# VectorE in GpSimd's place for the elementwise work of a hybrid mixer and mixture-of-experts block

## Chip and metric

One core of one Trainium2 chip. The metric is the device time of one execution in microseconds, the median of several runs. TensorE (PE) multiplies matrices out of SBUF into PSUM; VectorE (DVE) and ScalarE (ACT) read and write both; GpSimd (POOL) works on SBUF only and also issues the indirect DMAs; SyncE (SP) issues most other DMAs.

## What is computed

One layer of a hybrid block on 1024 tokens of width 1024, with 16 learnt tokens in front, all in float32:

```
h   = layer_norm([meta; x])
q,f,i,g,... = split(h @ w_in)                     # 9224 columns
y_a = head_norm(hgrn2(q, 1-f, i, log f)) * silu(g_a)          # 8 heads of 128
y_b = head_norm(mlstm(conv q, conv k, v)) * sigmoid(o_b)      # 4 heads
h   = layer_norm(alpha*h + (sigmoid(gate_a)*(y_a @ w_a) + sigmoid(gate_b)*(y_b @ w_b)) @ w_out)
out = layer_norm(alpha*h + routed_experts(h, top 8 of 64) + shared_expert(h))
```

HGRN2 is a gated linear recurrence: scores between a query at t and a key at s carry, for each of 128 channels, the product of the forget gates between s and t.

## The kernel before

**Precision and weights.** A float32 product is made of three matmuls of a faster format: each operand is a high part plus a low part, and high x high, high x low and low x high are added up in PSUM (`mm3`, L134 to L136). A weight piece of 128x1024 comes by DMA into a `wraw` tile, ScalarE copies it into the high part `wh` (L195), and the low part is raw minus high, `wl` (L196). `split_weights` does this for a list of pieces; `on_pool` names those whose low part GpSimd makes. `load_slab` splits four pieces, a slab of 512 columns, with high priority, so ahead of their use, and gives GpSimd pieces 1 and 3 (`SLAB_POOL`). The six pieces of the shared expert are split in the same way, 1, 3 and 5 of them on GpSimd (`SHARED_POOL`). The experts of the routed part never use GpSimd for this (`POOL_SPLITS` is empty, L1505).

**Stages.** The embedding makes the first norm and transposes it (L282 to L348); its own low parts and bias sums on GpSimd (L283, L325) are outside the change. Then for two halves of the HGRN part: a slab IA, a slab GA, a slab of f, one of q, and four heads. A slab goes through TensorE tile by tile into one of three PSUM banks `mm`, and from there through a staging tile to DRAM; heads load their parts from there. Then come VB and OB, the convolution, four mLSTM heads with the branch gates, the branch and output products by halves of the tokens with the second norm (`Tokens.norm`, L160 to L162), routing and the shared expert, the loop over 95 blocks of expert tokens, and the last norm.

**Gates.** `gate_out` (L413 to L425) turns a tile of GA into silu times a row of norm weights, a tile of OB into sigmoid times such a row. ScalarE writes the sigmoid to a staging tile (L419); for silu it also copies the PSUM tile to a second one (L422), and GpSimd multiplies twice (L423, L424) before SP's DMA to DRAM.

**A head.** `hgrn_head` builds the scores by doubling: at level lv blocks of B = 2^lv steps pair up. With `pre` the running product of gates within a block and `suf` that to a block's end, a level makes `qp` = query x pre of the odd blocks (L725), `ks` = key x suf of the even blocks (L727), 8 small matmuls (L739), a masked write of the scores (L742, or two ScalarE copies from level 5 on), the new suffix (L756) and the new prefix (L757). Level 0 is short (L719 to L721), level 6 ends the suffixes (L753, L754). Of levels 1 to 6 GpSimd makes the keys except at level 6 (`KS_DVE`), and of levels 1 to 5 the suffixes except at level 5 (`SUF_DVE`). Before the levels the diagonal is taken (L700 to L707); after them transposes, the chunk states (L779, L782), the output matmuls (L791, L792) into a PSUM tile `po` of which there is one, and the head norm (L794 to L799).

**Order.** The framework plans the order of instructions on each engine at build time, by priority in program order and by its own estimates of durations, and each engine then runs its list in that order, waiting on semaphores. A few parts are excepted, where the order is that of the program: PE and DVE in the embedding, PE in the branch and output stage and the first half of the token stage, PE, POOL and SP in the expert loop. In the heads all engines are planned, so a projection's matmuls fill the places between those of a head as the plan has them.

Of the kernel before, what the change touches and what calls it, by code (L numbers as in the profile page):

```python
# [14 lines left out]
AF = mybir.ActivationFunctionType  # L15
# [4 lines left out]
P = 128  # L20
D = 1024
KT = 8
# [22 lines left out]
KS_DVE = (6,)  # L45
SUF_DVE = (5,)
# [2 lines left out]
TAIL = (('A',1),('A',3),('S',0),('S',2),(('C0','C1'),()),('A',5),(('C2','C3','S4'),(0,1,2,3)),('F',0),('F',1),('A',7),('F',2),('F',3),('S',6),(('C4','C5','C6','C7'),(4,5,6,7)),('F',5),('F',4),('F',7),('F',6))  # L49
ADD_DVE = (3,5,7)  # L50
MUL_POOL = ()
ADD_POOL = (5,6,7)
SHARED_POOL = (1, 3, 5)
LATER = 300
RATE = 4.6
RATE_S = 3.0
# [9 lines left out]
SLAB_POOL = (1, 3)  # L66
# [4 lines left out]
def block_kernel(tc, A, out):  # L71
    nc = tc.nc
# [85 lines left out]
    def layer_norm(o, x, g, b, n, mul, add):  # L158
        sc = layer_norm_stats(x, n)
        nc.scalar.activation(o, x, AF.Identity, bias=sc[:n, 1:2], scale=sc[:n, 0:1])  # L160
        mul.tensor_mul(o, o, g[:n])
        add.tensor_add(o, o, b[:n])  # L162
# [22 lines left out]
    def split_weights(src, ahead, take=None, on_pool=()):  # L185

        res = []
        take = take or (lambda j: [wpool.tile([P, 1024], F32R, name="w" + q, tag="w" + q, bufs=6) for q in "hl"])
        with tc.high_priority(ahead) if ahead else ExitStack():
            for j, v in enumerate(src):  # L190
                raw = take_raw()
                dst = raw if len(v.shape) == 2 else raw.rearrange("p (k n) -> p k n", k=2)
                last.append(nc.sync.dma_start(dst, v))
                h, l = take(j)
                nc.scalar.activation(h, raw, AF.Copy)  # L195
                (nc.gpsimd if j in on_pool else nc.vector).tensor_sub(l, raw, h.bitcast(F32))  # L196
                res.append((h, l))
        return res
# [3 lines left out]
    def load_slab(src, c0):  # L202

        pairs = split_weights([src[k * 256:(k + 1) * 256, c0:c0 + 512].rearrange("(k p) n -> p k n", p=P)
                               for k in range(KT // 2)], 3000, on_pool=SLAB_POOL)
        hs = [t[:, c:c + 512] for t, _ in pairs for c in (0, 512)]
        ls = [t[:, c:c + 512] for _, t in pairs for c in (0, 512)]
        return hs, ls
# [40 lines left out]
    def stage_tile():  # L249
        return stage.tile([P, 512], F32, name="st", tag="st", bufs=6)  # L250
# [155 lines left out]
    def natural_slab(c0, emit, meta, slab=None):  # L406
        slab = slab or load_slab(w_in, c0)
        for i in range(NT):
            emit(proj_n(slab, NM + i * P, P), NM + i * P, P)
        if meta:  # L410
            emit(proj_n(slab, 0, NM), 0, NM)

    def gate_out(dst, c0, src, silu):  # L413
        row = stage.tile([P, 512], F32, name="nrow", tag="nrow", bufs=1)
        nc.sync.dma_start(row, bass.AP(tensor=src.tensor, offset=src.offset + c0, ap=[[0, P], [1, 512]]))

        def emit(pm, t0, n):
            s = stage_tile()
            nc.scalar.activation(s, pm, AF.Sigmoid)  # L419
            if silu:  # L420
                x = stage_tile()
                nc.scalar.activation(x, pm, AF.Copy)  # L422
                nc.gpsimd.tensor_mul(s, s, x)  # L423
            nc.gpsimd.tensor_mul(s, s, row)  # L424
            nc.sync.dma_start(dst[t0 - NM:t0 - NM + n, c0:c0 + 512], s)  # L425
        return emit

# [13 lines left out]
    def f_slab(s):  # L441
        slab = load_slab(w_in, FA + s * 512)
        for j in range(4):
            f = s * 4 + j
            for t0, n in GROUPS:
                pm = proj_t(slab, j, t0, n)
                st = stage_tile()
                nc.scalar.activation(st[:, :n], pm, AF.Sigmoid)
                nc.scalar.activation(st[:, :n], st[:, :n], AF.Identity, bias=lb[:, f:f + 1], scale=om[:, f:f + 1])
                nc.sync.dma_start(fT[f * P:(f + 1) * P, t0:t0 + n], st[:, :n])  # L450

    def q_slab(s):
        slab = load_slab(w_in, QA + s * 512)
        for j in range(4):
            f = s * 4 + j
            for g in range(2):
                pm = proj_t(slab, j, NM + g * 512, 512)
                st = stage_tile()
                nc.scalar.activation(st, pm, AF.Copy)
                nc.sync.dma_start(qT[f * P:(f + 1) * P, g * 512:(g + 1) * 512], st)  # L460
# [117 lines left out]
    def ps_sc():  # L578
        return psum.tile([P, 512], F32, name="sc", tag="sc", bufs=2)
# [7 lines left out]
    def rt(shape, tag, bufs=1, dt=F32):  # L587
        return rec.tile(shape, dt, name=tag, tag=tag, bufs=bufs)
# [88 lines left out]
    def hgrn_head(h, kss, st, zero):  # L677
# [12 lines left out]
        k = rt([P, L], "a2")  # L690
# [6 lines left out]
        kx = k[:, NM:L].rearrange("p (c t) -> p c t", t=P)  # L697
# [10 lines left out]
        for lv in range(7):  # L708
            B = 1 << lv
            N = 512 // B  # L710

            def sp(t):
                r = t.rearrange("p c (n w b) -> p (c n) w b", w=2, b=B)
                return r[:, :, 0, :], r[:, :, 1, :]

            p0, p1 = sp(pre)
            s0, s1 = sp(suf)
            if lv == 0:
                nc.gpsimd.tensor_copy(s0, p1)  # L719
                nc.gpsimd.memset(s1, 1.0)  # L720
                nc.vector.tensor_mul(p1, p1, p0[:, :, B - 1:B].to_broadcast([P, N, B]))  # L721
                continue
            qp = rt([P, N, B], "qp", 2)
            odd = [r.rearrange("p c (n w b) -> p c n w b", w=2, b=B)[:, :, :, 1] for r in (q, pre)]
            (nc.gpsimd if lv in QP_POOL else nc.vector).tensor_mul(qp.rearrange("p (c n) b -> p c n b", c=8), *odd)  # L725
            ks = kss[lv % 2]
            (nc.vector if lv in KS_DVE else nc.gpsimd).tensor_mul(sp(ks)[0], sp(kx)[0], s0)  # L727
            sc = ps_sc()
            qpf = qp.rearrange("p n b -> p (n b)")
            for c in range(8):  # L730
                t64 = c * 64
                if lv == 6:
                    spans = ((0, 64, 0, 64),)
                elif lv == 5:
                    spans = ((0, 32, 0, 32), (64, 96, 32, 64))
                else:
                    spans = ((0, P, 0, 64),)
                for a, b, u, v_ in spans:
                    nc.tensor.matmul(sc[a:b, t64 + u:t64 + v_], ks[:, c, a:b], qpf[:, t64 + u:t64 + v_],  # L739
                                     start=True, stop=True)  # L740
            if lv < 5:
                nc.vector.copy_predicated(sp(st)[1], lmask[:, lv].rearrange("p (n b) -> p n b", b=B),  # L742
                                          sc.rearrange("p (n b) -> p n b", b=B))
            else:
                scc = sc.rearrange("p (c t) -> p c t", t=64)
                if lv == 5:
                    nc.scalar.activation(st[0:32, :, 32:64], scc[0:32, :, 0:32], AF.Copy)
                    nc.scalar.activation(st[64:96, :, 96:128], scc[64:96, :, 32:64], AF.Copy)
                else:
                    nc.scalar.activation(st[0:64, :, 64:128], scc[0:64], AF.Copy)  # L750
            if lv == 6:

                nc.vector.tensor_mul(s1, s1, sp(kx)[1])  # L753
                nc.vector.tensor_mul(s0, sp(ks)[0], p1[:, :, B - 1:B].to_broadcast([P, N, B]))  # L754
            else:
                (nc.vector if lv in SUF_DVE else nc.gpsimd).tensor_mul(s0, s0, p1[:, :, B - 1:B].to_broadcast([P, N, B]))  # L756
            nc.vector.tensor_mul(p1, p1, p0[:, :, B - 1:B].to_broadcast([P, N, B]))  # L757
        nc.vector.tensor_mul(q, q, pre)
        pt = ps_tr()
# [284 lines left out]
    class Tokens:  # L1044
# [5 lines left out]
        def norm(self):  # L1050
            layer_norm(self.z, self.z, g_ln1, b_ln1, P, nc.gpsimd if self.i in MUL_POOL else nc.vector,
                       nc.gpsimd if self.i in ADD_POOL else nc.vector)
            nc.sync.dma_start(h1[self.i * P:(self.i + 1) * P, :], self.z)
# [157 lines left out]
    def after_out1(s, i):  # L1211
# [4 lines left out]
        if s == 1:  # L1216
            toks[4 + i].norm()
            if i == 3:
# [4 lines left out]
    pairs = split_weights([A["wshared"][:, j * 1024:(j + 1) * 1024] for j in range(6)], 3000,  # L1223
                          on_pool=SHARED_POOL)
    shared = [h for h, _ in pairs], [l for _, l in pairs]
# [233 lines left out]
    N = len(order)  # L1459
# [132 lines left out]
    with tc.tile_pool(name="ov", bufs=1) as ov:  # L1592
# [47 lines left out]
        with tc.For_i(0, n_blocks, 1) as b:  # L1640
# [6 lines left out]
            pm = work[:, 512:1024].rearrange("p (a b) -> p a b", b=64)  # L1647
# [208 lines left out]
```

## Time and profile before

| | us |
|---|---|
| median of 3 runs (2491.28 to 2496.71) | 2494.8 |
| profiled execution | 2498.45 |
| its span, first to last instruction | 2496.7 |
| TensorE busy | 2344.4 |
| VectorE busy | 1575.8 |
| ScalarE busy | 1107.3 |
| GpSimd busy | 762.1 |

The profile has a table of busy time by engine, busy time by stage with the clock that TensorE was granted (as a share of full speed), groups of instructions by source line, a table of waits and a timeline. A group's row gives line, engine, operation, the tile written and those read, the shape and the count, then busy time and mean duration in ns, then the engine's idle time just before these instructions and what ended it. Matmuls overlap, so a busy TensorE need not be at its peak. What ended a wait is inferred from semaphores.

### The profile page before, as it was taken

The numbers are of one execution on the slowest core, as the hardware profiler recorded it, in microseconds if no ns is written. First come the engines' busy times: TensorE is split into PE (matmuls) and PEld (weight loads), VectorE is DVE, ScalarE is ACT, GpSimd is POOL, SyncE is SP. The second block draws the span as 40 slices with busy tenths as digits, with TensorE's granted clock in tenths as the row PEclk, the third lists the DMA queues.
The fourth block names the chain that finished last, engine by engine and source line by source line (L and its number), as shares of the span: only waits on it lengthen the run. The fifth ranks groups of instructions, "written<-read, shape, count | busy, mean of one in ns | idle before, by whom it ended". The sixth has DMA issues, their size and how long they took to land. (4 is left out here: it accounts for less than half of the span.)

```text
span 2496.7 us, 35578 instructions
## 1 busy us (share of the span) xinstructions
PE 2344.4 (94%) x12754; PEld 1878.5 (75%) x12754; DVE 1575.8 (63%) x2967; ACT 1107.3 (44%) x1858; POOL 762.1 (31%) x454
## 2 busy tenths in 40 slices
PE   6999989999899999999999999999999999999991
PEld 4788877987787987778777777777777777777760
DVE  8342776147721556412468487788888887888884
ACT  3342122321222236422233231677777776777772
POOL 3442344234412100011121220233433434444432
PEclk8999998999999999999999999999999999999996
DMA  6233231423322245444545323899999999999984
GB/s 243 89 104 115 68 121 56 140 84 99 94 89 86 97 149 187 134 135 152 175 156 170 121 98 131 271 301 334 328 320 322 319 328 317 319 313 330 302 268 149
DMA packets 203058, 475.15 MB, mean 190 GB/s; under 512 B 18672, under 2 KB 67504, under 8 KB 202880
## 3 DMA queue, kind: packets, MB, share of 16 engines
q1 hardware_dynamic: 181040, 396.24, 45.7%
q0 software_dynamic: 21088, 73.94, 12.5%
q10 hardware_dynamic: 752, 2.69, 0.3%
q8 instruction: 101, 1.65, 0.3%
q14 instruction: 77, 0.63, 0.1%
HBM read 370.59 MB, written 102.20 MB: 189 GB/s over the span
## 5 line engine op out<-in xcount | busy, mean ns | idle before, releaser
L196 POOL TENSOR_TENSOR wl<-wraw,wh 128x1024 fp32r<-128x1024 f32 x59 | 166.1, 2820 | 659.1 <-ACT wh L195 617.3
L1438 POOL DMA_INDIRECT acc<-yo,idx x95 | 189.8, 1998 | 509.8 <-DMA acc<-yo,idx 104.9
L135 PE MATMUL mm<-hL,wh 128*128 128x512 f32 (+2 forms) x768 | 280.4, 365 | 0.0
L134 PE MATMUL mm<-hH,wh 128*128 128x512 f32 (+2 forms) x768 | 280.2, 365 | 0.0
L136 PE MATMUL mm<-hH,wl 128*128 128x512 f32 (+2 forms) x768 | 280.1, 365 | 0.0
L196 DVE TENSOR_TENSOR wl<-wraw,wh 128x1024 fp32r<-128x1024 f32 x59 | 101.9, 1727 | 279.9 <-ACT wh L195 275.4
L136 PE MATMUL mm<-wh,hL 128*128 128x512 f32 x512 | 209.4, 409 | 5.3 <-DVE hL L345 5.2
L135 PE MATMUL mm<-wl,hH 128*128 128x512 f32 x512 | 207.1, 404 | 3.0 <-DVE wl L283 3.0
L134 PE MATMUL mm<-wh,hH 128*128 128x512 f32 x512 | 209.2, 409 | 0.0
L134 PEld LDWEIGHTS mm<-hH,wh 128*128 128x128 f32 x768 | 146.2, 190 | 17.5 <-issue 1.3
L135 PEld LDWEIGHTS mm<-hL,wh 128*128 128x128 f32 x768 | 146.2, 190 | 16.3 <-issue 0.2
L136 PEld LDWEIGHTS mm<-hH,wl 128*128 128x128 f32 x768 | 146.4, 191 | 15.8 <-issue 0.2
L1359 POOL DMA_INDIRECT xg<-h,idx x95 | 140.2, 1476 | 53.9 <-issue 24.4
L1505 DVE TENSOR_TENSOR wl<-eraw,wh 128x1024 fp32r<-128x1024 f32 x112 | 134.9, 1216 | 15.8 <-ACT wh L1504 15.4
L195 ACT ACTIVATE wh<-wraw 128x1024 fp32r<-128x1024 f32 x118 | 122.3, 1056 | 49.6 <-PE mm L135 36.7
L1505 DVE TENSOR_TENSOR wl<-wraw,wh 128x1024 fp32r<-128x1024 f32 x96 | 115.8, 1216 | 27.3 <-ACT wh L1504 27.0
L134 PE MATMUL mm<-wh,xh 128*128 128x512 f32 (+3 forms) x296 | 124.2, 419 | 0.0
L1504 ACT ACTIVATE wh<-eraw 128x1024 fp32r<-128x1024 f32 x112 | 117.0, 1060 | 13.9 <-PE mm L136 9.3
L136 PEld LDWEIGHTS mm<-wh,hL 128*128 128x128 f32 x512 | 98.4, 192 | 29.4 <-DVE hL L345 8.3
L136 PE MATMUL mm<-wh,xl 128*128 128x512 f32 (+3 forms) x296 | 117.9, 398 | 0.0
L135 PE MATMUL mm<-wl,xh 128*128 128x512 f32 (+3 forms) x296 | 117.3, 396 | 0.0
L135 PEld LDWEIGHTS mm<-wl,hH 128*128 128x128 f32 x512 | 98.6, 193 | 24.4 <-DVE wl L283 3.5
(546 smaller groups left out, 5883.8 us busy)
## 6 DMA issues: line engine op xcount, KB each, us to landing
eraw<-in_wexp_dram SPq DMA_DIRECT2D x210, 512.0 KB, 8.2
wraw<-in_wexp_dram SPq DMA_DIRECT2D x168, 512.0 KB, 7.8
wraw<-in_w_in_dram SPq DMA_DIRECT2D x72, 512.0 KB, 4.5
sgT<-st SPq DMA_DIRECT2D x32, 256.0 KB, 3.1
sg<-sgT SPq DMA_DIRECT2D x32, 256.0 KB, 4.1
wraw<-in_w_branch_a_dram SPq DMA_DIRECT2D x16, 512.0 KB, 4.2
wraw<-in_w_branch_b_dram SPq DMA_DIRECT2D x16, 512.0 KB, 4.5
wraw<-in_w_out_dram SPq DMA_DIRECT2D x16, 512.0 KB, 4.3
```

The lines of the kernel that those rows point to most:

```text
L134: nc.tensor.matmul(o, ah, bh, start=start, stop=False)
L135: nc.tensor.matmul(o, ah, bl, start=False, stop=False)
L136: nc.tensor.matmul(o, al, bh, start=False, stop=stop)
L195: nc.scalar.activation(h, raw, AF.Copy)
L196: (nc.gpsimd if j in on_pool else nc.vector).tensor_sub(l, raw, h.bitcast(F32))
L1359: nc.gpsimd.indirect_dma_start(out=self.x, out_offset=None, in_=h1[:, :], in_offset=bass.IndirectOffsetOnAxis(ap=self.idx, axis=0))
L1438: self.out = nc.gpsimd.indirect_dma_start(out=acc[:, :], out_offset=bass.IndirectOffsetOnAxis(ap=self.idx, axis=0), in_=self.y, in_offset= ...
L1504: nc.scalar.activation(h, raw, AF.Copy)
L1505: (nc.gpsimd if j in POOL_SPLITS else nc.vector).tensor_sub(l, raw, h.bitcast(F32))
```

## The change

VectorE makes every low part of the mixer, branch, output and shared-expert weights, all keys and suffixes of the heads from level 1 on, the products of the gates, and the bias sum of the second norm for blocks 5 to 7. In the silu gate the ScalarE copy is gone: VectorE multiplies the sigmoid by the PSUM tile itself. GpSimd keeps the embedding's part, level 0 of the heads, fills, the last norm's sums and the indirect DMAs.

```diff
-ADD_POOL = (5,6,7)
-SHARED_POOL = (1, 3, 5)
+ADD_POOL = ()
+SHARED_POOL = ()
...
     def load_slab(src, c0):
         pairs = split_weights([src[k * 256:(k + 1) * 256, c0:c0 + 512].rearrange("(k p) n -> p k n", p=P)
-                               for k in range(KT // 2)], 3000, on_pool=SLAB_POOL)
+                               for k in range(KT // 2)], 3000)
...
             nc.scalar.activation(s, pm, AF.Sigmoid)
             if silu:
-                x = stage_tile()
-                nc.scalar.activation(x, pm, AF.Copy)
-                nc.gpsimd.tensor_mul(s, s, x)
-            nc.gpsimd.tensor_mul(s, s, row)
+                nc.vector.tensor_mul(s, s, pm)
+            nc.vector.tensor_mul(s, s, row)
...
-            (nc.vector if lv in KS_DVE else nc.gpsimd).tensor_mul(sp(ks)[0], sp(kx)[0], s0)
+            nc.vector.tensor_mul(sp(ks)[0], sp(kx)[0], s0)
...
-                (nc.vector if lv in SUF_DVE else nc.gpsimd).tensor_mul(s0, s0, p1[:, :, B - 1:B].to_broadcast([P, N, B]))
+                nc.vector.tensor_mul(s0, s0, p1[:, :, B - 1:B].to_broadcast([P, N, B]))
```

## Rows read from the trace of the kernel before

**Rows 1.** The page's busy table: us, share of the span, instructions.

```profile
PE 2344.4 (94%) x12754; PEld 1878.5 (75%) x12754; DVE 1575.8 (63%) x2967; ACT 1107.3 (44%) x1858; POOL 762.1 (31%) x454
```

**Rows 2.** Busy time by stage: us, PE, PEld, DVE, ACT, POOL, clock, DMA.

```profile
240.00:420.00 180.00, 161.92 (x1066) 136.20 (x1066) 132.51 (x287) 36.79 (x105) 76.56 (x51) 0.94 0.29 87
...
530.00:700.00 170.00, 154.74 (x1062) 129.29 (x1062) 127.81 (x289) 34.20 (x107) 70.95 (x46) 0.99 0.29 90
...
1610.00:2450.00 840.00, 829.11 (x4786) 618.13 (x4785) 690.27 (x1063) 605.66 (x946) 328.34 (x208) 1.00 0.98 311
```

**Rows 3.** Groups by line, GpSimd, whole span, shapes kept apart.

```profile
L196 POOL TENSOR_TENSOR wl<-wraw,wh 128x1024 fp32r<-128x1024 f32 x59 | 166.1, 2820 | 659.1 <-ACT wh L195 617.3 <-PE mm L136 39.5 <-DMA oB<-st 1.9
L727 POOL TENSOR_TENSOR kss<-a,a 128x512 f32<-128x512 f32 x40 | 64.9, 1622 | 48.7 <-DVE a L691 26.5 <-PE sc L739 20.2
L756 POOL TENSOR_TENSOR a<-a,a 128x512 f32<-128x512 f32 x32 | 52.8, 1648 | 52.5 <-DVE a L721 50.1 <-DVE a L757 0.7
L424 POOL TENSOR_TENSOR st<-st,nrow 128x512 f32<-128x512 f32 x32 | 45.4, 1420 | 60.5 <-ACT st L419 59.3
L423 POOL TENSOR_TENSOR st<-st 128x512 f32<-128x512 f32 x16 | 22.1, 1382 | 53.4 <-ACT st L422 53.4
...
L162 POOL TENSOR_TENSOR z<-z,b_ln 128x1024 f32<-128x1024 f32 x3 | 8.1, 2684 | 26.5 <-DVE z L161 20.0 <-DVE rs_t L125 6.5
```

**Rows 4.** Groups by line, VectorE, whole span, shapes kept apart.

```profile
L1505 DVE TENSOR_TENSOR wl<-eraw,wh 128x1024 fp32r<-128x1024 f32 x112 | 134.9, 1216 | 15.8 <-ACT wh L1504 15.4
...
L196 DVE TENSOR_TENSOR wl<-wraw,wh 128x1024 fp32r<-128x1024 f32 x59 | 101.9, 1727 | 279.9 <-ACT wh L195 275.4 <-PE mm L136 4.4
...
L725 DVE TENSOR_TENSOR qp<-a,a 128x512 f32<-128x512 f32 x48 | 50.3, 1048 | 0.8
...
L727 DVE TENSOR_TENSOR kss<-a,a 128x512 f32<-128x512 f32 x8 | 5.5, 683 | 0.0
```

**Rows 5.** TensorE's waits, 80 to 1610 us: total, times, longest.

```profile
PE po L791 <- DVE g L799: 12.3, 4, 4.9
PE sc L739 <- DVE qp L725: 6.9, 9, 0.9
PE sc L739 <- POOL a L756: 6.3, 6, 1.9
...
PE sc L705 <- DVE st L707: 3.8, 4, 1.0
PE sc L705 <- DVE a L700: 3.7, 5, 0.8
PE tr L559 <- DVE igr L546: 3.7, 1, 3.7
```

**Rows 6.** Timeline near 360 us, VectorE and TensorE: start, us, instruction, idle before.

```profile
354.27 2.69 DVE L196 TENSOR_TENSOR wl<-wraw,wh 128x1024 fp32r<-128x1024 f32 x1 [0.67 <-ACT wh L195]
...
365.18 0.80 PE L791 MATMUL po<-v,st 128*128 128x128 f32 x2 [4.94 <-DVE g L799]
```

**Rows 7.** Timeline from 1464 us, VectorE and GpSimd.

```profile
1464.38 1.56 DVE L123 TENSOR_TENSOR rs_t<-ln_sc 128x1 f32<-128x1 f32 x1
1465.97 2.33 DVE L125 TENSOR_TENSOR rs_t<-rs_t,rs_v 128x1 f32<-128x1 f32 x1
1468.33 2.33 DVE L127 SCALAR_TENSOR_TENSOR ln_sc<-rs_t,ln_sc 128x1 f32<-128x1 f32 x1
...
1465.88 4.76 POOL L196 TENSOR_TENSOR wl<-wraw,wh 128x1024 fp32r<-128x1024 f32 x2
```

**Rows 8.** Timeline from 981 us, VectorE and TensorE.

```profile
980.96 3.42 DVE L622 TENSOR_TENSOR a<-a,a 128x1024 f32<-128x1024 f32 x1
984.30 3.36 DVE L196 TENSOR_TENSOR wl<-wraw,wh 128x1024 fp32r<-128x1024 f32 x1
...
988.42 0.76 PE L608 MATMUL sc<-br,sel 36*128 36x512 f32 x1 [3.30 <-DVE a L621]
```

## Prediction

> **What bounds the kernel now.** I read the page's busy table first, then busy time by stage, then the table of what TensorE waited for, and last the instruction timelines of the places where it waited. TensorE is busy 94% of the span and VectorE 63% [rows 1]; that is an average over stages with different limits. The expert loop from 1610 to 2450 us keeps TensorE busy 829 of 840 us at full clock, GpSimd does nothing in it that the change moves (gathers, scatters, fills), and I price it at nothing; the same holds for the tail after it and for the embedding. The two stages of four HGRN heads each are different: 240 to 420 us has TensorE busy for 161.9 of 180 us with a mean granted clock of 0.94, 530 to 700 us for 154.7 of 170 us, and VectorE is busy there for 132.5 and 127.8 us [rows 2]. So up to 1610 us the time is TensorE's own work, which the change leaves alone, plus the stalls in it. What can move is the stalls.
>
> In the table of TensorE's waits [rows 5] the first three and both L705 rows belong to the heads: 12.3 + 6.9 + 6.3 + 3.8 + 3.7 = 33.0 us, 4.1 us for each of the 8 heads. Clock lost there, from the two window rows, is at most (1 - 0.94) x 161.9 + (1 - 0.99) x 154.7 = 9.7 + 1.5 = 11.2 us. Each engine runs a fixed order that was planned at build time with estimated durations; when an instruction comes later than planned, TensorE stands at it although projections that could fill the time are queued behind. A stall is therefore lateness against the plan, and the question is what makes VectorE and GpSimd late.
>
> **What the moved work does where it is.** While GpSimd runs an elementwise instruction, VectorE's own stand still. From 1464 us on three instructions over one column per partition take 1.56, 2.33 and 2.33 us; two GpSimd weight pieces run from 1465.88 for 4.76 us beside them [rows 7]. Near 360 us a weight piece takes 2.69 us on VectorE, and TensorE then stands 4.94 us at the output matmul of a head [rows 6]. At 981 us L622, a product of 128x1024, takes 3.42 us and the weight piece after it 3.36 us, beside a duration of 1.22 us for 128x1024 that nothing disturbs; TensorE stalls 3.30 us just after [rows 4, 8]. By lines: the weight piece on VectorE averages 1.727 us in the mixer where GpSimd takes the other half, and 1.216 us in the expert loop where GpSimd takes none; the query product L725 averages 1.048 us where the same shape at L727 needs 0.683 [rows 4]. So where the two engines meet, a piece moved over costs VectorE 1.22 us, less than the 1.5 to 2.2 us that it lost by standing beside it.
>
> The Trainium skill, "SBUF — State Buffer", section "Who interferes with whom", says that a VectorE instruction with two SBUF inputs and a GpSimd instruction that reads SBUF exclude each other for the whole instruction, whoever starts first. By that rule every such excess vanishes and the sum below would go to its far end, 44 us less; the instructions of 2.33 us agree with it [rows 7]. The same skill's "Perfetto Trace Analysis", section "Optimizing Scalar/DVE Operations", speaks against the change: it says a saturated VectorE may be worth unloading, even to GpSimd, though it doubts the gain because of that port. By its first half the time would be that of the second rival below, with its chance.
>
> **What is removed and added, part by part.** GpSimd loses 166.1 + 64.9 + 52.8 + 45.4 + 22.1 + 8.1 = 359.4 us [rows 3]. VectorE gains 59 weight pieces x 1.216 = 71.7 us, 40 keys and 32 suffixes x 0.683 = 49.2 us, 32 + 16 gate products x 0.683 = 32.8 us (half a row of the same size; the products that now read PSUM have no row, I take the same), and 3 bias sums x 1.216 = 3.6 us: 157 us. It gives back 59 x (1.727 - 1.216) = 30.1 us on pieces and 48 x (1.048 - 0.683) = 17.5 us on L725, and the smaller excesses of rows 6 to 8. So VectorE becomes some 100 us busier in 1500 us. That is no bound by itself; the places are.
>
> *Heads.* A head's VectorE gets 5 keys (levels 1 to 5) and 4 suffixes (levels 1 to 4), 9 x 0.683 = 6.1 us, and gives back 17.5 / 8 = 2.2 us: 3.9 us more on VectorE. For that, GpSimd's chain of 9 instructions of 1.62 and 1.65 us [rows 3] and its handovers go. If the plan could not absorb it, 8 x 3.9 = +31 us would land on TensorE; if every stall goes, -33.0. Of the 33.0 us, 6.3 wait for GpSimd itself, 6.9 for L725 and 12.3 for the output product L799 that rows 6 show delayed by GpSimd: 25.5 us that have their cause in the coincidence; the 7.5 us of L705 have none that I see. The new order is planned with durations that will be true, but it has VectorE as the only engine for everything; I take a little over half of the 25.5: -14 us, and of the clock the same share of 33, 14 / 33 x 11.2 = -5 us (ends 0 and -11.2).
>
> *Other stalls.* At 981 us VectorE loses 2.20 + 2.14 = 4.34 us and would pay 2 x 1.216 = 2.43: 1.9 us earlier at the instruction TensorE waits for, -2 us (ends 0 and -3.3). In the norms near 1470 us it loses at most 1.56 + 2.33 + 2.33 = 6.2 us [rows 7] and pays two pieces and one bias sum, 3.6: -2 us (ends +1 and -4; the LN stages are where VectorE has no slack, and the sums of the two later blocks have to fit in too). The stall of 3.7 us for L546 after the gate scans [rows 5] has gate products and pieces put into the same VectorE stretch, and the disturbance taken out; I take 0 (ends -3.7 and +4, three more gate products and two pieces).
>
> *Gates and slabs.* The silu path drops one ScalarE copy; the projection's PSUM bank, of three, is now held until VectorE's product has read it. VectorE's queue there holds head steps, scans and pieces; behind a gate product that waits for its sigmoid stand a head's keys. Ends 0 and 16 x 0.683 = +11 us; with three banks nearer to the first: +2. All four pieces of a slab now queue on one engine, 4 x 1.216 = 4.9 us, against two on GpSimd of 2.82 us each, 5.6 us beside two on VectorE: the slab is ready no later. TensorE's waits show none for a mixer piece [rows 5], being loaded ahead; what queues behind a piece that waits for its ScalarE half is a head step. Ends 0 and +10; I take +2. The gates' output DMA leaves SP's queue a little earlier, at no gain.
>
> Sum: -14 - 5 - 2 - 2 + 0 + 2 + 2 = -19 us. The profiled execution took 2498.45 us (span 2496.7 and 1.75 around it), 3.65 above the median of 2494.8. 2498.45 - 19 - 3.65 = 2475.8: I forecast **2476 us**, 0.75% less.
>
> **Rivals.**
> One: *stalls only change their place*. TensorE is the bound, its order is planned anew, and a plan with a busier VectorE leaves as many late arrivals as it removes. For it: 7.5 us of the waits in heads have nothing to do with GpSimd. Against: the largest do. The heads give 0, the clock 0, the rest 0: 2495 us, within 2490 to 2500. Chance 0.17.
>
> Two, *slower*: VectorE's queue becomes what the heads wait for. Place: levels 1 to 5 of each head, where scores, keys, suffixes, products and predicated copies now stand in one queue, with pieces and gate products of the next stage between them. VectorE is busy for 260 of 350 us in the two stages; 8 x 3.9 = 31 us and the net of gates and slabs there bring it over 83%. If half of the 31 us appears as TensorE stalls and only the 6.3 us that wait for GpSimd are saved, the heads give +9 us in place of -19, and gates and slabs at the middle of their ends +10 in place of +4, less 4: +15, some 2510 us; with all of it 2525. It decides once TensorE's stalls per head grow beyond the present 4.1 us. Chance 0.17.
>
> Three: *the change doesn't shorten anything on VectorE*, because the long instructions are long for another reason than GpSimd; then VectorE carries the 157 us whole, 6.1 us a head, and the second rival's place decides with a greater price, some 2515 us. The coincidences in rows 6 to 8 speak against it. Chance 0.05.
>
> **How the numbers follow.** Forecast 0.61, rivals 0.17, 0.17, 0.05. The forecast's own range: all of 25.5 + 11.2 + 3.3 + 4 = 44 us gained gives 2451, a gain of only 6 us 2489. The whole range runs from 2452 to 2508, which holds the second rival's milder half. Some 0.2%, 5 us, is what a measurement of this kernel can tell from no change; so faster 0.61, same 0.17, slower 0.22.
>
> **What would show it.** In the profile of the changed kernel: L196 on VectorE 118 times at about 1.22 us, L725 near 0.69, no small instruction above 1 us in the norms; VectorE some 90 us busier than its 1575.8, GpSimd some 360 us less busy. The head rows among TensorE's waits should add up to some 19 us with no entry of 4 us, the clock of both head stages should be 0.98 or better. I am wrong if waits for L727, L756 or L725 on VectorE add up to over 33 us, if a gate product holds a bank and TensorE waits for it, or if the durations on VectorE do not fall.

## The result, and the profile after

The changed kernel takes 2424.8 us (2422.78 to 2428.05, 5 runs) against 2494.8: a ratio of 0.9719, with an interval of 0.9705 to 0.9733. That is 70 us less, where 19 were forecast, and outside the range. The profiled execution took 2424.22 us with a span of 2422.4. From line 424 on, a line of before has a number lower by 2 in after.

The page's busy table of after, which answers to [rows 1]:

```profile
PE 2318.0 (96%) x12754; PEld 1856.0 (77%) x12754; DVE 1609.1 (66%) x3149; ACT 1098.7 (45%) x1841; POOL 402.2 (17%) x272
```

TensorE runs the same 12754 instructions. The span is 2496.7 - 2422.4 = 74.3 us shorter. Of that, TensorE's idle time gives 47.9 (2496.7 - 2344.4 = 152.3 before, 2422.4 - 2318.0 = 104.4 after) and its busy time 26.4. GpSimd lost 359.9 us of work. VectorE took on 157 us of it (the sum that the prediction worked out) and is busier by only 33.3.

Where the time went, by stage. Both kernels are cut at the same instructions of the program (so at different times); columns are stretch, length, then busy us with instructions of PE, PEld, DVE, ACT, POOL, then granted clock, DMA share, GB/s. The stages are: up to the first f slab, heads 0 to 3, heads 4 to 7, the mLSTM heads, the branch gates, the half of tokens that follows the first branch stage, routing, and the expert loop. Before:

```profile
83.10:158.50 75.40, 69.35 (x328) 57.51 (x327) 30.87 (x37) 36.16 (x54) 45.52 (x27) 0.95 0.25 82
158.50:486.10 327.60, 309.52 (x1871) 272.00 (x1871) 157.41 (x324) 85.93 (x187) 115.28 (x76) 0.97 0.33 99
486.10:813.20 327.10, 311.84 (x1750) 256.29 (x1749) 152.00 (x319) 68.05 (x153) 113.20 (x68) 0.99 0.30 96
...
919.60:1053.80 134.20, 128.97 (x578) 98.66 (x578) 73.62 (x200) 72.94 (x178) 5.78 (x2) 0.97 0.50 164
1053.80:1170.60 116.80, 113.70 (x491) 91.30 (x492) 16.17 (x17) 27.65 (x39) 15.55 (x6) 0.97 0.38 125
...
1309.60:1472.40 162.80, 155.83 (x730) 127.05 (x728) 113.87 (x302) 48.15 (x66) 34.49 (x13) 0.98 0.42 138
1472.40:1572.20 99.80, 88.99 (x513) 71.50 (x513) 76.20 (x256) 20.24 (x41) 9.88 (x8) 0.91 0.32 116
1572.20:2422.00 849.80, 843.54 (x4912) 632.09 (x4912) 712.54 (x1097) 622.64 (x965) 328.00 (x208) 1.00 1.00 318
```

The same stages of after:

```profile
82.80:153.20 70.40, 69.43 (x318) 53.92 (x317) 34.86 (x55) 31.11 (x45) 13.46 (x13) 1.00 0.29 93
153.20:457.10 303.90, 302.18 (x1881) 265.82 (x1880) 171.20 (x386) 81.91 (x181) 6.06 (x9) 1.00 0.34 106
457.10:770.00 312.90, 309.73 (x1750) 254.42 (x1749) 172.06 (x381) 67.78 (x153) 3.63 (x6) 1.00 0.31 101
...
875.80:1003.70 127.90, 126.69 (x580) 97.06 (x580) 71.69 (x202) 71.55 (x172) 0.00 (x0) 1.00 0.51 171
1003.70:1114.00 110.30, 109.06 (x484) 87.62 (x485) 20.22 (x23) 27.48 (x39) 0.00 (x0) 1.00 0.40 133
...
1253.10:1402.20 149.10, 148.07 (x717) 121.99 (x716) 107.12 (x292) 48.37 (x66) 0.00 (x0) 1.00 0.43 146
1402.20:1496.90 94.70, 86.74 (x528) 69.98 (x527) 74.45 (x269) 20.38 (x41) 7.12 (x6) 0.96 0.33 121
1496.90:2347.00 850.10, 843.02 (x4911) 632.32 (x4911) 712.83 (x1097) 623.07 (x965) 323.00 (x208) 1.00 0.99 318
```

The eight heads give 23.7 + 14.2 = 37.9 us. As much comes from places that the prediction priced at nearly nothing: 5.0 before the heads, 6.3 in the mLSTM heads, 6.5 in the branch gates, 13.7 in the token half, 5.1 in routing. The expert loop stays where it was, as forecast. The mean granted clock rises to 1.00, the upper of TensorE's two levels (1.2 and 2.4 GHz), in the first six of these stages. In heads 0 to 3 TensorE stands 303.90 - 302.18 = 1.7 us in all, where it stood 18.1.

The longest of what TensorE still waited for from 80 to 1510 us in after (total, times, longest), to set against [rows 5]:

```profile
PE sc L703 <- DVE a L698: 3.5, 5, 1.0
PE po L1486 <- DVE oh L1471: 3.1, 1, 3.1
PE tr L170 <- DVE xl L173: 2.8, 1, 2.8
```

The five head rows summed to 33.0 us in before; 3.5 is left. The output product, the query product and GpSimd's suffix have gone from the list, and so has the wait for the gate scans.

VectorE's groups of after, by line and shape, to set against [rows 4]:

```profile
L196 DVE TENSOR_TENSOR wl<-wraw,wh 128x1024 fp32r<-128x1024 f32 x118 | 141.6, 1221 | 202.2 <-ACT wh L195 197.9 <-PE mm L136 3.7 <-DMA sg<-sgT 0.3
L723 DVE TENSOR_TENSOR qp<-a,a 128x512 f32<-128x512 f32 x48 | 33.2, 691 | 0.2
L754 DVE TENSOR_TENSOR a<-a,a 128x512 f32<-128x512 f32 x40 | 27.6, 690 | 0.4
```

One small norm line and one small head line, with the shortest, median and longest duration in ns, first in before and then in after:

```profile
L125 DVE TENSOR_TENSOR rs_t<-rs_t,rs_v x111: 143/161/2325, 10.1 to 1480.3; 128x1 f32<-128x1 f32 x48, 128x4 f32<-128x4 f32 x48, 128x8 f32<-128x8 f32 x12, 16x1 f32<-16x1 f32 x3
L795 DVE TENSOR_SCALAR ss<-ss x16: 170/438/1840, 270.0 to 699.4; 128x4 f32<-128x4 f32 x16
```

```profile
L125 DVE TENSOR_TENSOR rs_t<-rs_t,rs_v x111: 147/161/168, 9.9 to 1407.6; 128x1 f32<-128x1 f32 x48, 128x4 f32<-128x4 f32 x48, 128x8 f32<-128x8 f32 x12, 16x1 f32<-16x1 f32 x3
L793 DVE TENSOR_SCALAR ss<-ss x16: 169/170/172, 268.6 to 682.3; 128x4 f32<-128x4 f32 x16
```

L795 of before is L793 of after. The longest L125 fell from 2.325 us, one of those in [rows 7], to 0.168, the longest of the head line from 1.840 to 0.172.

### The profile page after: what moved, and what is told of

Same layout as the page of the kernel before. It is cut to its first block, busy times and chain, and to the rows that moved or that the text cites. A ratio compares the mean times of both kernels' runs of the same rounds, so it can differ in the third digit from the quotient of the medians.

```text
span 2422.4 us, 35454 instructions
## 1 busy us (share of the span) xinstructions
PE 2318.0 (96%) x12754; PEld 1856.0 (77%) x12754; DVE 1609.1 (66%) x3149; ACT 1098.7 (45%) x1841; POOL 402.2 (17%) x272
## 5 line engine op out<-in xcount | busy, mean ns | idle before, releaser
L196 DVE TENSOR_TENSOR wl<-wraw,wh 128x1024 fp32r<-128x1024 f32 x118 | 141.6, 1221 | 202.2 <-ACT wh L195 197.9
L135 PEld LDWEIGHTS mm<-hL,wh 128*128 128x128 f32 x768 | 144.4, 188 | 16.5 <-issue 0.5
L136 PEld LDWEIGHTS mm<-hH,wl 128*128 128x128 f32 x768 | 144.6, 188 | 15.6 <-issue 0.2
L1503 DVE TENSOR_TENSOR wl<-wraw,wh 128x1024 fp32r<-128x1024 f32 x96 | 115.8, 1216 | 27.6 <-ACT wh L1502 27.3
L134 PEld LDWEIGHTS mm<-wh,hH 128*128 128x128 f32 x512 | 97.9, 191 | 21.2 <-PE mm L529 0.8
```

What stands on the lines that cost most here:

```text
L134: nc.tensor.matmul(o, ah, bh, start=start, stop=False)
L135: nc.tensor.matmul(o, ah, bl, start=False, stop=False)
L136: nc.tensor.matmul(o, al, bh, start=False, stop=stop)
L1503: (nc.gpsimd if j in POOL_SPLITS else nc.vector).tensor_sub(l, raw, h.bitcast(F32))
```

## The experiments

Two theories are set against each other. **Standing** (the expectations call it exclusion): while a GpSimd elementwise instruction runs, VectorE's instructions stand; that makes VectorE late, and the lateness reaches TensorE. **Handover:** what cost the time were the chains that crossed from VectorE to GpSimd and back, with their semaphores and GpSimd's own longer durations; taking the crossings away is the gain. Ratios and "less" are against the kernel before. The code cuts shorten the definitions of tiles, and three dots stand for lines left out.

**One part of the change at a time.** First the heads alone:

```diff
-            (nc.vector if lv in KS_DVE else nc.gpsimd).tensor_mul(sp(ks)[0], sp(kx)[0], s0)
+            nc.vector.tensor_mul(sp(ks)[0], sp(kx)[0], s0)
...
-                (nc.vector if lv in SUF_DVE else nc.gpsimd).tensor_mul(s0, s0, ...)
+                nc.vector.tensor_mul(s0, s0, ...)
```

> The kernel before with the keys and suffixes of the heads alone moved to VectorE; weight pieces, gate products and bias sums stay on GpSimd. Exclusion theory (GpSimd's instructions stop VectorE's at times that the plan does not know): the 72 moved instructions account for the small stalls of the heads (6.9 + 6.3 of 33.0 us), the pieces and gates beside the heads for the 4 long ones; so some 20 us of the 70 gained, 2475 us. Handover theory (the heads wait for GpSimd's results, 4.1 us of stalls each): nearly all of the 38 us that the two head stages lost goes here, 2455 us. Sum theory of the prediction: -14 us for heads, 2480.

Measured: 2478.1 us, ratio 0.9925 (0.9909 to 0.9942), 18.5 less, as the standing theory had it. Every crossing of the heads from level 1 on is gone (the copy and the fill of level 0 stay on GpSimd), and a quarter of the gain is there. VectorE's groups show why it isn't more; keys, then query products:

```profile
L727 DVE TENSOR_TENSOR kss<-a,a 128x512 f32<-128x512 f32 x48 | 39.5, 823 | 0.0
L725 DVE TENSOR_TENSOR qp<-a,a 128x512 f32<-128x512 f32 x48 | 37.5, 781 | 0.3
```

Both need 0.684 to 0.691 us in after. GpSimd's weight pieces and gate products still run beside the heads.

The slabs alone, low parts of all mixer and shared-expert pieces on VectorE:

```diff
-SHARED_POOL = (1, 3, 5)
+SHARED_POOL = ()
...
-                               for k in range(KT // 2)], 3000, on_pool=SLAB_POOL)
+                               for k in range(KT // 2)], 3000)
```

> The kernel before with the low parts of weights alone moved to VectorE (59 pieces); keys, suffixes, gate products and bias sums stay on GpSimd. Exclusion theory: the pieces are GpSimd's longest instructions (2.8 us each) and stand beside the long stalls at 365, 651 and 988 us and the norms; 25 to 35 us faster, some 2465. Handover theory: TensorE waited for no piece of the mixer, so no gain, 2490 to 2500.

Measured: 2453.4 us, 0.9833 (0.9817 to 0.985), 43 less: the largest single part, and more than the 25 to 35 expected. The busy table and the weight piece's group:

```profile
PE 2325.3 (95%) x12754; PEld 1859.8 (76%) x12754; DVE 1570.9 (64%) x3026; ACT 1103.0 (45%) x1855; POOL 593.0 (24%) x395
...
L196 DVE TENSOR_TENSOR wl<-wraw,wh 128x1024 fp32r<-128x1024 f32 x118 | 146.5, 1263 | 266.4 <-ACT wh L195 262.4 <-PE mm L136 3.7
```

VectorE makes 59 pieces more and is busy 4.9 us *less* than in before: 59 x 1.216 = 72 us were added and 77 came back.

The gates alone, and the three bias sums alone:

```diff
-                x = stage_tile()
-                nc.scalar.activation(x, pm, AF.Copy)
-                nc.gpsimd.tensor_mul(s, s, x)
-            nc.gpsimd.tensor_mul(s, s, row)
+                nc.vector.tensor_mul(s, s, pm)
+            nc.vector.tensor_mul(s, s, row)
```

> The kernel before with the gate products alone moved to VectorE, ScalarE's copy of the silu path gone. Exclusion theory: 48 instructions of 1.3 us, of which about a quarter fall beside heads; 3 to 10 us faster, some 2488. Handover theory: nobody on TensorE waits for them, 0. The prediction had +2 us here for PSUM banks held longer.

```diff
-ADD_POOL = (5,6,7)
+ADD_POOL = ()
```

> The kernel before with the bias sum of the second norm for blocks 5 to 7 alone moved to VectorE. Exclusion theory: three instructions of 2.4 to 3.3 us beside a chain of short VectorE instructions, 3.6 us paid for up to 6 gained; 2 to 6 us faster, 2490. Prediction: -2.

Measured: the gates 2479.6 us, 0.9929 (0.9913 to 0.9946), 17 less where 3 to 10 were expected, with VectorE busier by 16.5 us for 32.8 us of added products; the sums 2490.4 us, 0.9975 (0.9964 to 0.9986), 6 less, with VectorE 4.0 us less busy although three instructions were added. The four parts sum to 18.5 + 43 + 17 + 6 = 84.5, more than the whole's 70: some of the same waits go with either part. TensorE's wait for the output product, 12.3 us in before [rows 5], is 2.9 us with the heads alone, 3.0 with the slabs alone and 6.0 with the gates alone.

And the whole change without the heads (after, with keys and suffixes put back on GpSimd as in before):

```diff
-            nc.vector.tensor_mul(sp(ks)[0], sp(kx)[0], s0)
+            (nc.vector if lv in KS_DVE else nc.gpsimd).tensor_mul(sp(ks)[0], sp(kx)[0], s0)
...
-                nc.vector.tensor_mul(s0, s0, ...)
+                (nc.vector if lv in SUF_DVE else nc.gpsimd).tensor_mul(s0, s0, ...)
```

> The changed kernel with keys and suffixes of the heads put back on GpSimd as they were before; all else on VectorE. Exclusion theory: the small stalls of the heads come back (13 us and some clock), 2440 us. Handover theory: the two head stages come back whole, +38 us, 2463 us. If the parts add up, this one and the heads alone together make the 70 us.

Measured: 2440.5 us, 0.9784 (0.9767 to 0.9802). The heads are worth 15.6 us as the last part and 18.5 as the first. Its busy table:

```profile
PE 2325.1 (95%) x12754; PEld 1860.9 (76%) x12754; DVE 1589.1 (65%) x3077; ACT 1098.2 (45%) x1841; POOL 520.0 (21%) x344
```

VectorE is 20.0 us *less* busy here than in after, and the kernel is slower. So VectorE's total is not what is paid; that the plan counts on VectorE's own instructions and not on the standing would explain this, but no run separates it. TensorE's waits for a suffix on GpSimd itself are 2.9 us here (6.3 in before). How the rest of the 15.6 us divides between standing, GpSimd's longer instructions and the new plan is not shown.

**GpSimd work that nobody waits for.** These five kernels are after with GpSimd instructions added whose output nobody reads. TensorE, VectorE, ScalarE and SyncE run after's lists of instructions in after's order, so the plan can't differ, and no result of GpSimd's is handed back. A buffer that such an instruction reads still comes free later. With the product ghosts no wait of these four engines between 80 and 1530 us is put down to a ghost; with the slab ghosts SyncE's loads of weights wait for one 8 times, 17.8 us in all, while TensorE waits for no weight there; with the fills ScalarE waits for one, 4.8 us in the heads' kernel and 1.4 in the slabs'. First, useless products next to the keys (each of the key's input and the key itself):

```diff
+    ghost = ...   # nc.gpsimd.tensor_mul(ghost tile, u, w), twice (once at level 5)
...
-            nc.vector.tensor_mul(sp(ks)[0], sp(kx)[0], s0)
+            nc.vector.tensor_mul(sp(ks)[0], sp(kx)[0], s0); lv < 6 and ghost(lv, ks, sp(kx)[0], sp(ks)[0])
```

> The changed kernel, and beside each key on VectorE at levels 1 to 5 GpSimd again does two products of 128x512 (one at level 5), of the key's inputs, whose result nobody reads: 72 instructions as before the change. The order of instructions on TensorE, VectorE, ScalarE and SP is the same as in the changed kernel, instruction for instruction. Exclusion theory: VectorE's instructions are lengthened again, the heads' stalls come back though nobody waits for GpSimd: 15 to 35 us slower than the changed kernel, 2440 to 2460. Handover theory: nothing waits, so 2425 within 3 us.

Measured: 2468.6 us, 0.989 (0.9874 to 0.9907): 44 us more than after, and more than the 35 at most expected. Its busy table, the groups that changed, the ghosts, and TensorE's waits from 80 to 1530 us:

```profile
PE 2338.4 (95%) x12754; PEld 1868.6 (76%) x12754; DVE 1670.0 (68%) x3149; ACT 1097.3 (44%) x1841; POOL 521.2 (21%) x344
...
L755 DVE TENSOR_TENSOR a<-a 128x512 f32<-128x512 f32 x48 | 51.9, 1081 | 1.0
L754 DVE TENSOR_TENSOR a<-a,a 128x512 f32<-128x512 f32 x40 | 45.3, 1134 | 0.4
...
L674 POOL TENSOR_TENSOR ghost<-a,kss 128x512 f32<-128x512 f32 x72 | 113.6, 1578 | 307.6 <-DVE kss L725 281.5 <-DVE km L691 21.3 <-DVE km L693 2.2
...
PE sc L703 <- DVE a L698: 16.0, 6, 3.0
PE sc L737 <- DVE qp L723: 9.9, 14, 1.6
PE sc L737 <- DVE kss L725: 6.4, 10, 1.1
```

The suffix and prefix products that follow a key go from 0.690 to 1.134 and 1.081 us. VectorE is 60.9 us busier with the same list. TensorE's waits for it come back, and its busy time rises by 20.4 us beside 28.4 us more idle time (2471.2 - 2338.4 = 132.8 against 104.4).

Second, the same GpSimd time in fills: in the ghost's place a copy of one column, which ties it to the same moment, and six fills (three at level 5).

```diff
+    ghost = ...   # nc.gpsimd.tensor_copy(ghost[:, 0:1], ks[:, 0, 0:1]), then nc.gpsimd.memset(ghost, 0.0) x6 (x3)
```

> The same as the kernel with the useless products, but GpSimd fills its tile instead (after one copy of one column, which times it), six fills of 128x512 at levels 1 to 4 and three at level 5: about the same busy time, reads of SBUF gone. Again the same order on all other engines. If GpSimd's reading is what excludes VectorE: 2425 within 4 us. If any work of GpSimd does, or its semaphores: as slow as the kernel with the products.

Measured: 2432.4 us, 0.9748 (0.9731 to 0.9764): 7.6 more than after. The same two groups, and the fills:

```profile
L755 DVE TENSOR_TENSOR a<-a 128x512 f32<-128x512 f32 x48 | 33.1, 690 | 1.0
L754 DVE TENSOR_TENSOR a<-a,a 128x512 f32<-128x512 f32 x40 | 27.6, 690 | 0.4
...
L674 POOL MEMSET ghost<- 128x512 f32 x216 | 113.5, 525 | 12.5
```

113.5 us of fills leave suffix and prefix at 0.690 us; VectorE is 4.1 us busier. So it isn't GpSimd's being busy at that place that stretches VectorE: it is its instructions that read tensors in SBUF.

The 7.6 us are outside the 4 expected, but most of them are not the fills' doing. TensorE's list is the same, so the start of the same matmul can be compared in the two profiled executions. At 134 us it comes 1.0 us earlier than in after, at 153 us 5.8 us later, and the first fill starts at 174.9. From there to the end of the heads the lag grows by 2.5 us, to 8.3. The rows of that early stretch, after and then the fills, show why:

```profile
134.00:151.00 17.00, 17.00 (x73) 12.17 (x73) 7.19 (x13) 7.69 (x9) 3.29 (x5) 1.00 0.35 102
134.00:151.00 17.00, 17.00 (x39) 10.24 (x39) 2.95 (x10) 3.17 (x4) 3.28 (x5) 0.51 0.16 47
```

The clock stood at its lower level here, though TensorE had been busy all of the 14 us before in both; why it fell is not shown. The same fall is in the profiled execution with the product ghosts, before the first of them: 6.8 of the 48.8 us by which its span is longer come from there, and 42.8 arise in the heads.

Third, the same pair for the weight slabs: a useless raw minus high for pieces 1 and 3 of the slabs of `w_in`, and in its place a one-column copy with five fills.

```diff
-                (nc.gpsimd if j in on_pool else nc.vector).tensor_sub(l, raw, h.bitcast(F32))
+                nc.vector.tensor_sub(l, raw, h.bitcast(F32)); j in on_pool and nc.gpsimd.tensor_sub(ghostw, raw, h.bitcast(F32))
...
-                               for k in range(KT // 2)], 3000)
+                               for k in range(KT // 2)], 3000, on_pool=SLAB_POOL if src is A["w_in"] else ())
```

> The changed kernel, and GpSimd again subtracts high part from raw for pieces 1 and 3 of each slab of the input projection, into a tile that nobody reads (the branch, output and shared-expert pieces have none): 30 odd instructions of 2.4 us and more; same order of instructions on TensorE, VectorE, ScalarE and SP as in the changed kernel. Exclusion theory: 8 to 20 us slower than the changed kernel, 2433 to 2445. Handover theory: 2425 within 3 us.

> The changed kernel; at pieces 1 and 3 of the slabs of the input projection, where GpSimd's useless differences cost 53 us, it copies one column of the high part and then fills 128x512 five times: it holds the high part's slot a little and is as long busy, but reads almost nothing. Same order of instructions on TensorE, VectorE, ScalarE and SP as in the changed kernel. Exclusion theory: 2425 to 2435, as the fills in the heads (2432). If holding the weight slots or GpSimd being busy made the 53 us: 2460 or more.

Measured: 2478.4 us, 0.9918 (0.9891 to 0.9945), 53.5 more than after where 8 to 20 were expected (four runs from 2469 to 2488; the profile is of the slowest); with fills 2428.7 us, 0.9728 (0.9705 to 0.9751), not told apart from after. The weight piece and the ghosts, first with reads, then with fills:

```profile
L196 DVE TENSOR_TENSOR wl<-wraw,wh 128x1024 fp32r<-128x1024 f32 x118 | 206.9, 1775 | 197.7 <-ACT wh L195 193.0 <-PE mm L136 3.7 <-DMA sg<-sgT 0.3
L196 POOL TENSOR_TENSOR ghostw<-wraw,wh 128x1024 bf16<-128x1024 f32 x32 | 97.3, 3041 | 588.4 <-ACT wh L195 508.4 <-DMA hx<-hX 73.6 <-issue 4.6
```

```profile
L196 DVE TENSOR_TENSOR wl<-wraw,wh 128x1024 fp32r<-128x1024 f32 x118 | 141.7, 1221 | 202.5 <-ACT wh L195 198.0 <-PE mm L136 3.7
L196 POOL MEMSET ghostw<- 128x512 f32 x160 | 85.4, 534 | 9.1
```

32 GpSimd instructions make VectorE 68.5 us busier (1677.6 against 1609.1) and give the weight piece about the mean that it had in before, 1.775 against 1.727 us [rows 4].

Fourth, the dose: 40 useless products in place of the 72 (one at each of levels 1 to 5).

> The changed kernel with one useless product on GpSimd beside each key at levels 1 to 5, 40 in place of 72; same order of instructions on the other engines. Exclusion theory, lateness in proportion to the time read beside VectorE: 40 / 72 of the 44 us that the 72 cost, +24, 2449 us. If the plan's slack took up the first part of a delay, less than half: 2430 to 2440.

Measured: 2439.8 us, 0.977 (0.9753 to 0.9787), 15 more than after, with VectorE 33.5 us busier. VectorE's loss follows the dose (63.6 us of ghosts against 113.6, 33.5 against 60.9). The time doesn't: 0.45 us for each us that VectorE loses, against 0.72 with the full dose. So the forecast in proportion, 2449 us, is missed, and the other one, that slack takes up the first part of a delay (2430 to 2440), holds. In the profiled executions the full dose has 28.4 us more idle time on TensorE than after and stretches of the lower clock in both head stages (mean granted clock 0.98 in each), half the dose 8.1 us and none there (1.00).

**What is left.** The last norm's sums moved to VectorE too, and then also the embedding's low parts, its bias sums and scalings, and the copy of level 0:

```diff
-ADD_DVE = (3,5,7)
+ADD_DVE = (0,1,2,3,4,5,6,7)
```

> The changed kernel with the last norm's five remaining bias sums on VectorE in one instruction with the scaling, in place of ScalarE's scaling and GpSimd's sum. Exclusion theory: in the changed kernel's tail three VectorE instructions of 1.28 us take 3.1, 2.3 and 2.3 us beside GpSimd's sums; 5 x 1.28 us added, as much or more given back, and the last two sums of 2.8 us each go: 3 to 6 us faster than the changed kernel, 2420. Sum of VectorE's work alone: +6 us, 2431.

```diff
-HX_DVE = (0, 1)
+HX_DVE = (-1, 0, 1, 2, 3, 4, 5, 6, 7)
...
-            (nc.gpsimd if j % 4 in SLAB_POOL else nc.vector).tensor_sub(l, raw[j], h.bitcast(F32))
+            nc.vector.tensor_sub(l, raw[j], h.bitcast(F32))
...
-                nc.gpsimd.tensor_copy(s0, p1)
+                nc.vector.tensor_copy(s0, p1)
```

> The kernel with the tail on VectorE, and besides the embedding's low parts and bias sums (scaling and sum in one instruction) and the heads' copy at level 0: no elementwise arithmetic left on GpSimd. Exclusion theory: the embedding has 8 norms whose centring takes 2.13 us for 1.22 and a stall of 3 us at its second weight piece; 2 to 6 us more than the tail alone, 2415. Against it: VectorE is busy there 64 of 83 us, and seven instructions of 1.28 us and four of 1.22 come on; +3 us, 2423.

Measured: the tail 2420.1 us, 0.9684 (0.9665 to 0.9704), the fastest of all kernels here and ahead of after's interval, if barely. Two VectorE instructions of the last norm in after, and the same two in the tail kernel:

```profile
2398.26 3.12 DVE L1726 SCALAR_TENSOR_TENSOR zf<-zf,fsm,wraw 128x1024 f32<-128x1024 f32 x1
2401.30 2.30 DVE L1707 TENSOR_SCALAR fr<-fr 128x4 int32<-128x4 int32 x1
```

```profile
2403.29 1.27 DVE L1726 SCALAR_TENSOR_TENSOR zf<-zf,fsm,wraw 128x1024 f32<-128x1024 f32 x1
2404.48 0.16 DVE L1707 TENSOR_SCALAR fr<-fr 128x4 int32<-128x4 int32 x1
```

Of the tail's gain only a part is standing: in after GpSimd's last sums were also on the chain that ended last (`POOL zf L1735`, some 10 us of it), and VectorE makes them faster. With the embedding as well it is 2427.1 us, 0.9718 (0.9701 to 0.9735), no better than after and slower than either forecast. In the embedding TensorE's wait for L345, the low part of the norm's transposed output, is 7.5 us there, 6.6 in the tail kernel and 5.4 in after, and its wait for L533 is 2.5 us against 0.8 and 0.6: VectorE comes later in that stage. TensorE reaches the end of the embedding 2.9 us later than in the tail kernel. The rest of the 7 us is not settled: the two profiled spans are only 2.1 us apart, with mean clocks of 0.985 and 0.984, while the other three runs of this kernel, at 2427 us and more, had 0.982.

## Why the prediction was wrong

**The mechanism was right.** GpSimd lost 359.9 us, 359.4 predicted. L196 runs 118 times at 1.221 us, the query product at 0.691, and the norm line shown above never exceeds 0.17 us. The ghosts show the cause without any change of plan: GpSimd instructions that read stretch VectorE by 60.9 and 68.5 us and the kernel by 44 and 53.5; fills of about the same time leave VectorE's durations as they were and cost some 4 us or less once the early fall of the clock is taken out. Handover falls as the main cause: no ghost hands anything back, and removing the crossings in the heads gave 18.5 of 70. What the changed plan adds on the way from before to after, beside the shorter instructions, was not separated.

The Trainium skill, "SBUF — State Buffer", section "Who interferes with whom", says that a VectorE instruction with two SBUF inputs contends with a GpSimd instruction that reads SBUF, not with one that only writes. The fills agree with that: 4.1 and 0.7 us of VectorE's time against 60.9 and 68.5. In before one stretched line, L795, has a single tensor input, which this sentence does not cover: at 358.01 us it takes 1.83 us beside a GpSimd weight piece and ends with it, at 359.8 (shown below).

**The failed step is the price of the stalls and of the clock lost with them.** In the prediction's sum standing time is -14 for the heads, -2, -2 and 0 for other stalls and +2 and +2 for gates and slabs, -14 together, and the clock is -5. Measured, TensorE's idle time fell by 47.9 us and its busy time by 26.4. Every one of these terms was too small or of the wrong sign. The four paragraphs that follow take them in turn, beginning with what stands behind them.

**What VectorE gives back.** The prediction took 157 us added, 47.6 us back on two lines (30.1 on L196, 17.5 on L725) "and the smaller excesses", and expected VectorE some 90 us busier. It is 33.3 us busier: 124 us came back. Compared shape by shape between the two kernels, VectorE's groups name some 105 of them: 47 on those two lines, as predicted, and 58 on some 25 others. The three norm lines L123, L125 and L127 lose 17 us together, L795 6.8, the branch product L1024 6.0, and the rest up to some 3 us each. They stood in the trace of before as groups with too long a mean or too long a maximum; [rows 7] showed three such instructions, and the prediction used them for one place instead of adding up their like. One long stall is followed to such pieces in the next paragraph; for the others that is the likely reading, not shown one by one.

**Stalls.** Heads: 25.5 us were put down to the coincidence and "a little over half" taken, -14, with 7.5 us of L705 left out because they "have none that I see". 29.5 went, L705 included. That half was a choice with no row behind it. The prediction also says that [rows 6] show the output product delayed by GpSimd; they show a long weight piece 11 us earlier and no GpSimd instruction. The nearer causes are in the head norm just before the stall ends, VectorE first, then GpSimd:

```profile
358.01 1.83 DVE L795 TENSOR_SCALAR ss<-ss 128x4 f32<-128x4 f32 x1
360.87 1.17 DVE L123 TENSOR_TENSOR rs_t<-ss 128x4 f32<-128x4 f32 x1
362.27 1.11 DVE L127 SCALAR_TENSOR_TENSOR ss<-rs_t,ss 128x4 f32<-128x4 f32 x1
...
357.41 2.40 POOL L196 TENSOR_TENSOR wl<-wraw,wh 128x1024 fp32r<-128x1024 f32 x1
360.76 1.26 POOL L423 TENSOR_TENSOR st<-st 128x512 f32<-128x512 f32 x1 [0.95 <-ACT st L422]
362.10 1.26 POOL L424 TENSOR_TENSOR st<-st,nrow 128x512 f32<-128x512 f32 x1
```

Three instructions of four columns, 0.16 to 0.17 us where nothing is beside them, end within 0.03 us of a weight piece and of the two products of a gate. They lose 3.6 us on the way to the output product, for which TensorE stands 4.94. So this stall hangs on the slabs and the gates, which the prediction priced apart from it. The other stalls were priced at -2, -2 and 0 by looking at three places; idle time outside the five head rows fell by 47.9 - 29.5 = 18.4 us.

**Gates and slabs** were the term of the wrong sign: +2 and +2. Alone they give 17 and 43 us less. The prediction asked whether VectorE's queue could hold them and not what their GpSimd versions did to VectorE; but the 59 weight pieces, 166 us of GpSimd's time [rows 3], were also the largest part of what GpSimd did beside VectorE; the weight piece on VectorE alone gave back 30 of the 124 us.

**Clock.** -5 us, at most 11.2, was worked out from two windows [rows 2]. TensorE's busy time fell by 26.4 us with the same instructions. By the clock that the trace records, before runs at 1.2 GHz in 15 stretches between 80 and 1600 us, 71.7 us in all, and after in 2, 10.2 us; half of the difference, 31 us, is about what the busy time lost. Only 24 of the 71.7 us lie in the two head stages, where the prediction looked. 14 of the 15 begin during one of TensorE's longer waits or right behind it: one at 362.3 us, in the wait of 4.94 us of [rows 6], one at 986.9, in that of 3.30 us of [rows 8]. Both of after's come with a wait of about 3 us. In the product ghosts idle and busy time came back together, 28.4 and 20.4 us, although some 7 us of the latter belong to the fall before the first ghost, and that fall, with TensorE busy all of the 14 us ahead of it, shows that waits aren't the only occasion. So the clock belongs in the price of a long stall: here 47.9 us of idle time went with 26.4 of busy time.

**The rivals.** *Stalls only change their place* fell: 33.0 to 3.5 us in the head rows, and no new row of that size took their place. *VectorE's queue* fell: 0.4 us a head where it needed more than 4.1. It is as full as that rival said, though: in after VectorE is busy 291 of 362 us over the heads themselves (236 to 420 and 500 to 678 us), 80%, where the rival had over 83%, and TensorE is hardly kept waiting. *No duration shortens* fell with L196 and L725.

The Trainium skill, "Perfetto Trace Analysis", section "Optimizing Scalar/DVE Operations", says that a saturated VectorE may be unloaded even to GpSimd, though with doubts. These runs bear out the doubts: 360 us of GpSimd's help saved VectorE 33 us, and the kernel without it is 70 us faster.

**Why TensorE feels an engine that is 63% busy.** In the ghost kernels each us that VectorE loses costs the kernel 0.72 us (43.8 / 60.9), 0.78 (53.5 / 68.5), or 0.45 at the half dose, by the median times. By the spans of the profiled executions, from which VectorE's figures come, it is 0.80 (48.8 / 60.9, or 0.70 without the fall of the clock before the first ghost), 0.93 (63.4 / 68.5) and 0.31 (10.3 / 33.5). From before to after it is 70 / 124 = 0.56. TensorE is the bound and takes its list in order, so it stands at whatever comes late, even when later work in its list is ready. Why the ratio lies anywhere between 0.3 and 0.9 stays open.

## What to carry to other kernels

Before GpSimd is given elementwise work, or when it has some, compare the mean and the longest duration of *each* VectorE group with those of the same shape in a stretch without GpSimd, the small ones too, and add up the excess: that sum, not GpSimd's busy time, is what VectorE pays. What reaches the kernel was 0.3 to 0.9 of it here. GpSimd work that only writes, such as fills, stayed cheap beside VectorE here. When an argument says that a stall's cause goes away, halving it needs a row that shows what comes late next: here 29.5 of 33.0 us went, and lost clock with them. A difference of a few us between two kernels can be a fall of the clock ahead of the edit: compare the start of the same matmul before crediting it.

## What was not expected of the hardware

An engine with more work can be less busy: with 59 more pieces of 1.22 us, in the kernel with the slabs alone, VectorE's busy time fell by 4.9 us; in before its weight piece took 1.73 us on average. Instructions over a single column were hit hardest for their size, 0.16 us becoming 2.33 [rows 7], and so was one with a single tensor input of four columns (L795, 0.17 to 1.84 us). In these runs GpSimd's reading arithmetic does this and its fills do not: 216 fills of 0.525 us left 0.690 us at 0.690. Nor does what it does in the expert loop: beside 328 us of gathers, scatters and fills [rows 2] VectorE's weight piece keeps 1.216 us [rows 4].
